# The first branch's values as pairs of half-size products, with the decays between the first pairs

## The chip, the cores and the metric

The kernel runs on one core of a Trainium2 chip. The metric is the device time of one execution in microseconds (us), as a median over runs. Engines are named as in the profile: PE (TensorE, matmuls), PEld (its weight loads), DVE (VectorE), ACT (ScalarE), POOL (GpSimd) and SP (SyncE, which issues nearly all DMAs here). SBUF is the on-chip memory, PSUM the banks into which PE writes its results.

## The reference, cut to what matters

One layer with two token mixers. A row-normalised x (1024 tokens, 1024 columns) goes through one wide input projection w_in, whose columns are cut into parts:

```python
h = rmsnorm(x, norm_g)
proj = h @ w_in
(g_q, g_k, g_v, g_gate, g_rank, s_q, s_k, s_v, s_gate, m_logits) = split(proj)

log_a = log_sigmoid(g_rank @ w_dec_up + b_dec) / 16          # the decays, per key channel
o_gla = gla_chunked(g_q, g_k, g_v, log_a)                    # first branch, 4 heads, dk 128, dv 256
o_gla = rmsnorm(o_gla, gla_norm_g) * silu(g_gate)
o_sb  = stick_breaking(s_q, s_k, s_v) * silu(s_gate)         # second branch, 8 heads, d 128
gates = sigmoid(m_logits + b_gate)
out = rmsnorm(x + (gates_a * (o_gla @ w_pa) + gates_b * (o_sb @ w_pb)) @ w_o, final_g)
```

In the first branch the cumulated decay e1 = exp(cumsum(log_a)) multiplies q, and e2 = exp(-cumsum(log_a)) multiplies k, with the sum started anew in each chunk of 64 tokens. The values g_v (4 heads of 256 columns) are used in chunks as they are.

## The kernel before, in words

All products run in a reduced-width float type (fp32r). To keep the accuracy of fp32, each operand x is cut by `split` (L152 to L154) into a high part, written by an ACT copy, and a low part, written by a DVE subtraction; a product is then three matmuls, high-high, high-low, low-high. h is kept transposed as four quarters `hq[n, e]`, by halves of the tokens (n) and by even and odd blocks of 128 rows (e), each as a high and a low tile of 128 x 4 x 512.

The kernel multiplies with w_in in two ways.

*Value units* (`proj_n`, `v_unit`). One unit takes 128 tokens and 256 columns: 8 row blocks x 3 = 24 matmuls with 256 columns each, with a block of h as the stationary operand, so that tokens lie on the partitions of the result. ACT and DVE split the result into a staging tile, and SP stores two units at a time. The line `st` holds 56 such units: three pairs of the second branch's heads (keys "s", 1 to 3; pair 0 was done while x was read), then the first branch's four heads (keys "g"), 8 units each. `store_v` writes the second branch's values to `d_v`; the first branch's go to `d_gv[h]`, as 128 tokens x 8 token blocks x (high, low) x 256 columns.

*Pairs* (`pair_job`, class `Pairs`). 256 columns of w_in are multiplied with all 1024 tokens by Strassen's scheme in Winograd's form: seven products instead of eight, each of half size in both row parity and token half, on combined operands. On the side of h these are the quarters A11, A12, A22 and the sums S1 to S4, built once and kept; on the side of w_in the four sub-blocks and the differences T1 to T4, built for every job. One product (a *unit*, numbered 0 to 6 in a job) is 4 row blocks x 3 = 12 matmuls with 512 columns each, with w_in as the stationary operand, so that the *columns of w_in* lie on the partitions of the result: the result is transposed as against a value unit's. Three PSUM banks x, y, z collect the products: units 0, 2, 4 and 6 add up in x, units 3 and 5 in z, unit 1 in y. Partial sums s1, s2 and s5 are copied out by ACT (`keep`, L260) before the bank goes on; `evict` then handles the four results (J, n): column block J, token half n. `total` (L291) adds the kept sum by DVE. `Pairs.run` also issues, at given units, the splits of the next job's weights and the load (and the four POOL subtractions for T1 to T4) of the one after that. Two raw weight buffers are there.

The order before:

1. x is read, normalised and transposed, with the values of the first pair of second-branch heads (to about 45 us).
2. The value stretch: 56 value units. Threaded between them in an order written by hand for ACT and DVE (`tc.manual_schedule`) are first the decays, then the sums for S1 to S4. The decays are seven steps: `code` (transposes of the rank code, L488), `logit` (the rank product on PE, bias by DVE, L495), `decay_a` (DVE, then Exp on ACT), `decay_b` (Ln on ACT, then DVE), `decay_c` (a scan on DVE, L507), `decay_d` (two Exp on ACT), `decay_e` (a small copy, and the stores of e1 and e2 to DRAM). Their tiles lie in the slots that later hold S1 to S4. The sums are made by POOL (L526, L529) one per unit, 32 in all, and each is split three units later. The line of sums has 36 entries.
3. 24 pair jobs, 168 units. The first 24 units run alone; the rest run four at a time between the 32 blocks (4 heads x 8 blocks of 128 tokens) of the first branch's recurrence (`gl_load`, `gl_local`, `gl_out`, `gl_gate`), and the last ones alone.
4. The second branch's attention, with gate and output projections between, then the second output projection and the final norm.

Outside of the hand-written stretches a planner orders each engine's instructions: it takes what is ready by its own cost estimates, and of several ready ones the one issued earlier in the text. On the chip each engine then works strictly through its planned list, and waits where an operand is not there. Tiles come from rings of a fixed number of buffers per tag: "f" (5 tiles of 128 x 512), "o" (3 staging tiles of 128 x 2 x 512), "tr" (2 PSUM banks for transposes), "pp" (3 PSUM banks for products).

Of the kernel before, what the change touches and what calls it, by code (L numbers as in the profile page):

```python
# [9 lines left out]
F32 = mybir.dt.float32  # L10
F32R = mybir.dt.float32r
AF = mybir.ActivationFunctionType
# [38 lines left out]
class Line:  # L51


    def __init__(self, items):
        self.items = list(items)
# [9 lines left out]
class Pairs:  # L65
# [1 line left out]

    def __init__(self, jobs):  # L70
        self.jobs = [j() for j in jobs]
        self.at = 0
# [22 lines left out]
def hybrid_layer(ctx: ExitStack, tc: tile.TileContext, x, norm_g, w_in, w_up, b_dec,  # L95
# [56 lines left out]
    def split(src, hi, lo, eng=nc.vector):  # L152
        nc.scalar.activation(hi, src, AF.Copy)  # L153
        eng.tensor_sub(lo, src, hi.bitcast(F32))  # L154

    def half(n):
        return slice(n * HALF, (n + 1) * HALF)
# [39 lines left out]
    def proj_n(ws, quads, tb, n=DV):  # L197

        pt = ps.tile([P, HALF], F32, tag="pp", name="pp", bufs=3)
        cs = slice(tb % 4 * P, (tb % 4 + 1) * P)  # L200
        for kb in range(KB):
            q = quads[tb // 4, kb % 2]
            h_, l_ = q[0][:, kb // 2, cs], q[1][:, kb // 2, cs]
            whi, wlo = ws(kb)
            nc.tensor.matmul(pt[:, 0:n], h_, whi, start=kb == 0, stop=False)  # L205
            nc.tensor.matmul(pt[:, 0:n], h_, wlo, start=False, stop=False)  # L206
            nc.tensor.matmul(pt[:, 0:n], l_, whi, start=False, stop=kb == KB - 1)  # L207
# [120 lines left out]
    def store_v(key, i, tb):  # L328

        st = vst.pop((key, tb // 2)) if tb % 2 else None  # L330
        if st is not None:
            for e in range(2):
                nc.sync.dma_start(d_v[2 * i + e][:, tb - 1:tb + 1], st[:, :, :, e * P:(e + 1) * P].bitcast(F32))

    def v_stage(key, tb):
        if tb % 2 == 0:
            vst[key, tb // 2] = (stage().rearrange("p a b -> p (a b)")
                                 .rearrange("p (t s c) -> p t s c", t=2, s=2))
        return vst[key, tb // 2][:, tb % 2]
# [91 lines left out]
        split(vraw[key][:, 4 * i:4 * i + 4], hi, lo)  # L431
        vws.setdefault(key, []).append((hi, lo))

    def v_unit(key, tb):
        nm, i = key
        st = v_stage(key, tb)
        split(proj_n(rows_of(vws[key]), hq, tb), st[:, 0], st[:, 1])
        if nm == "s":
            store_v(key, i, tb)
        elif tb % 2:  # L440
            nc.sync.dma_start(d_gv[i][:, tb - 1:tb + 1], vst.pop((key, tb // 2)).bitcast(F32))
# [21 lines left out]
    nc.sync.dma_start(wup, w_up)  # L463
    wst = slot(4, [P, GLA_H * P], "wst", F32R)
    rst = slot(5, [P, T], "rst", F32R)
    rmask = slot(7, [P, T], "rmask")
    nc.gpsimd.memset(wst.bitcast(F32), 0.0)
    nc.gpsimd.memset(rst.bitcast(F32), 0.0)
    nc.gpsimd.memset(rmask, 1.0)
    nc.gpsimd.memset(ch3(rmask)[:, :, 0:1], 0.0)  # L470
    u2 = [slot(i, [P, 2 * T], "u") for i in range(2)]
    e2 = [slot(i, [P, 2 * T], "e") for i in (2, 3)]
    U = [u2[h // 2][:, h % 2 * T:(h % 2 + 1) * T] for h in range(GLA_H)]
    E = [e2[h // 2][:, h % 2 * T:(h % 2 + 1) * T] for h in range(GLA_H)]

    def stack(dst, src, rows):
        for r0, part in zip((0, 32, 64), rows):
            if part == "h":
                nc.scalar.activation(dst[r0:r0 + RANK], src, AF.Copy)
        r0 = 32 * rows.index("l")  # L480
        nc.vector.tensor_sub(dst[r0:r0 + RANK], src, dst[0:RANK].bitcast(F32))

    def code(n):
        if n == 0:
            stack(wst, wup, "hlh")
        pt = ps.tile([P, HALF], F32, tag="tr", name="tr")
        for b in range(4):
            nc.tensor.transpose(pt[0:RANK, b * P:(b + 1) * P], rcode[:, n * 4 + b], ident)  # L488
        stack(rst[:, half(n)], pt[0:RANK, :], "hhl")

    def logit(h):
        for n in range(2):
            pt = ps.tile([P, HALF], F32, tag="tr", name="tr")
            nc.tensor.matmul(pt, wst[:, h * P:(h + 1) * P], rst[:, half(n)], start=True, stop=True)
            nc.vector.tensor_scalar(U[h][:, half(n)], pt, vcol[:, 16 + h:17 + h], None, op0=ALU.add)  # L495


    def decay_a(h):
        nc.vector.scalar_tensor_tensor(E[h], U[h], -1.0, U[h], op0=ALU.mult, op1=ALU.min)
        nc.scalar.activation(E[h], E[h], AF.Exp)  # L500

    def decay_b(h):
        nc.scalar.activation(E[h], E[h], AF.Ln, bias=1.0)
        nc.vector.scalar_tensor_tensor(E[h], U[h], 0.0, E[h], op0=ALU.min, op1=ALU.subtract)

    def decay_c(h):
        nc.vector.tensor_tensor_scan(U[h], rmask, E[h], 0.0, op0=ALU.mult, op1=ALU.add)  # L507

    def decay_d(h):
        nc.scalar.activation(E[h], U[h], AF.Exp, scale=1.0 / TAU)  # L510
        nc.scalar.activation(U[h], U[h], AF.Exp, scale=-1.0 / TAU)

    def decay_e(h):
        nc.vector.tensor_copy(ebl[:, h], ch3(E[h])[:, :, CH - 1])
        nc.sync.dma_start(d_e1[h], E[h])
        nc.sync.dma_start(d_e2[h], U[h])


    f = {}
# [33 lines left out]
    st.run(1)  # L553
    for i, s in enumerate("hl"):
        nc.sync.dma_start(d_a21[i], hq[1, 0][i].bitcast(F32))
    for fn, hs in ((code, ((0,), (1,))), (logit, ((0, 1), (2, 3))), (decay_a, ((0, 1), (2, 3))),
                   (decay_b, ((0,), (1,), (2,), (3,))), (decay_c, ((0,), (1,), (2,), (3,))),
                   (decay_d, ((0,), (1,), (2,), (3,))), (decay_e, ((0, 1, 2, 3),))):
        for group in hs:
            for h in group:  # L560
                fn(h)
            st.run(1)
    for ops in line:
        for op in ops:
            op()
# [33 lines left out]
    def merge_pair(c0, i, b0, dst):  # L599
# [14 lines left out]
    pairs = Pairs(gla_qk(0) + [gg_pair(0), merge_pair(C_MA, 0, 0, d_ga), gg_pair(1)] + gla_qk(1) +  # L614
                  [gg_pair(2), gg_pair(3)] +
                  [f for i in range(4) for f in (qk_pair(C_SQ, i, d_q), qk_pair(C_SK, i, d_k))] +
                  [merge_pair(C_MA, i, 0, d_ga) for i in range(1, 4)] +
                  [merge_pair(C_MB, i, 8, d_gb) for i in range(4)])
    pairs.run(24)


    gl_ctx = ExitStack()
# [449 lines left out]
```

## Time and profile before

| | |
|---|---|
| median of 3 runs | 1263.05 us (1262.35 to 1263.29) |
| profiled execution, its own time | 1259.98 us |
| its span (first to last instruction) | 1258.3 us |
| granted TensorE clock, mean | 0.999 |
| PE / DVE / ACT / POOL busy | 98% / 60% / 41% / 19% of the span |
| DMA | 212.09 MB, mean 169 GB/s |

The busy times come from one profiled execution. A matmul's row gives its full passage through the array, so rows of matmuls that follow each other overlap; the distance between two starts is what one costs in a row of many. "L254" is line 254 of the kernel above. A row of a group gives busy time, mean duration in ns, the idle time of the engine before its members, and what ended that idle time.

### The profile page before, as it was taken

To read this page: it belongs to the slowest core of one execution; us is meant where nothing else is said; L and a number is where in the kernel's file an instruction comes from. 1 tells how busy PE (TensorE), PEld (TensorE's weight loads), DVE (VectorE), ACT (ScalarE), POOL (GpSimd) and SP (SyncE) were. 2 spreads that over 40 slices of the span, in tenths; PEclk is the share of its full clock that TensorE was granted. 3 is DMA by queue.
4 is the path that set the end of the run, shared out by engine and by line. 5 is a ranking of instruction groups with operands and counts; after the bars stand their busy time and mean duration, and the time that the engine had idled before them with its cause. 6 is when DMAs were issued, how large, how long until landed. Compare 5 with 4: busy or idle time off the path is not lost.

```text
span 1258.3 us, 18805 instructions
## 1 busy us (share of the span) xinstructions
PE 1234.0 (98%) x6947; PEld 1054.5 (84%) x6947; DVE 753.4 (60%) x1309; ACT 519.8 (41%) x1024; POOL 243.3 (19%) x280
## 2 busy tenths in 40 slices
PE   8999999999999999999999999999999999999998
PEld 8999999888888888888888877777777878888986
DVE  5682454545667666666564357778887775444533
ACT  5454332344344444444444444545644443122322
POOL 2400471323223233232323010000100000000010
PEclk9999999999999999999999999999999999999999
DMA  7547353534644565655433765444775437543232
GB/s 270 186 142 269 126 181 133 188 116 149 192 157 137 188 208 173 215 179 177 159 117 121 246 206 160 135 163 147 220 245 175 135 109 265 190 161 110 85 116 92
DMA packets 176982, 212.09 MB, mean 169 GB/s; under 512 B 11222, under 2 KB 129004, under 8 KB 174332
## 3 DMA queue, kind: packets, MB, share of 16 engines
q1 hardware_dynamic: 175740, 209.34, 50.8%
q10 hardware_dynamic: 1152, 1.57, 0.3%
q8 instruction: 54, 0.88, 0.3%
q14 instruction: 36, 0.29, 0.1%
HBM read 133.28 MB, written 77.59 MB: 168 GB/s over the span
## 4 chain that ended last, share of the span: by engine, by line
PE 84%; DVE 8%; DMA 3%; ACT 2%; issue 2%; SPq 0%; POOL 0%; DVEq 0%; POOLq 0%; ACTq 0%
PE pp L254 12%; PE pp L256 12%; PE pp L255 12%; PE pp L207 7%; PE pp L205 7%; PE pp L206 7%; PE pp L193 6%; PE pp L194 6%; PE pp L192 5%; DVE eb L828 3%; PE av L864 1%; DVE be L833 1%; PE tr L847 1%; PE av L865 1%; PE av L863 1%
## 5 line engine op out<-in xcount | busy, mean ns | idle before, releaser
L153 ACT ACTIVATE wh<-raw 128x1024 fp32r<-128x1024 f32 x57 | 60.4, 1060 | 125.8 <-PE pp L193 69.6
L154 DVE TENSOR_TENSOR wl<-tt,wh 128x1024 fp32r<-128x1024 f32 x48 | 58.8, 1224 | 69.3 <-ACT wh L153 69.1
L291 DVE TENSOR_TENSOR f<-pp,f 128x512 f32<-128x512 f32 x72 | 49.7, 690 | 81.2 <-PE pp L256 77.9
L154 DVE TENSOR_TENSOR wl<-raw,wh 128x1024 fp32r<-128x1024 f32 x57 | 78.2, 1371 | 29.4 <-ACT wh L153 28.4
L153 ACT ACTIVATE wh<-tt 128x1024 fp32r<-128x1024 f32 x48 | 50.9, 1061 | 75.7 <-PE pp L255 69.0
L830 POOL TENSOR_SCALAR_AFFINE_SELECT be<-be 128x128 f32<-128x128 f32 x64 | 23.0, 360 | 277.1 <-ACT be L822 211.1
L828 DVE TENSOR_TENSOR_SCAN eb<-eb 128x128 f32<-128x128 f32 (+6 forms) x56 | 71.8, 1282 | 5.6 <-ACT eb L821 3.1
L154 DVE TENSOR_TENSOR o<-pp,o 128x256 fp32r<-128x256 f32 (+1 forms) x72 | 32.4, 451 | 66.1 <-ACT o L153 63.0
L153 ACT ACTIVATE o<-pp 128x256 fp32r<-128x256 f32 (+1 forms) x72 | 29.0, 403 | 93.5 <-PE pp L207 90.3
L821 ACT ACTIVATE eb<-z 128x384 f32<-128x384 f32 (+4 forms) x96 | 48.4, 506 | 44.6 <-PE z L819 30.7
L260 ACT ACTIVATE f<-pp 128x512 f32<-128x512 f32 x72 | 42.5, 590 | 55.8 <-PE pp L256 55.8
L228 POOL TENSOR_TENSOR tt<-raw 128x512 f32<-128x512 f32 x24 | 31.2, 1302 | 150.4 <-DVE wl L154 135.8
L153 ACT ACTIVATE ath<-tr 128x512 fp32r<-128x512 f32 (+2 forms) x96 | 44.0, 496 | 38.8 <-PE tr L847 37.9
L215 POOL TENSOR_TENSOR r<-r,nhalf 128x1 f32<-128x1 f32 x40 | 23.4, 586 | 188.3 <-DVE r L214 188.3
L154 DVE TENSOR_TENSOR atl<-tr,ath 128x512 fp32r<-128x512 f32 (+2 forms) x96 | 51.1, 546 | 5.3 <-ACT ath L153 5.3
L864 PE MATMUL av<-atl,v 128*128 128x256 f32 x160 | 47.0, 293 | 3.9 <-DVE atl L154 3.9
L847 PE MATMUL tr<-ident,be 128*128 128x128 f32 x288 | 44.5, 278 | 5.8 <-DVE be L833 4.9
L847 PEld LDWEIGHTS tr<-ident,be 128*128 128x128 f32 x288 | 32.5, 140 | 20.7 <-DVE be L833 11.2
L192 PE MATMUL pp<-bh,wh 128*128 128x512 f32 x128 | 49.9, 390 | 0.0
L193 PE MATMUL pp<-bl,wh 128*128 128x512 f32 x128 | 49.9, 390 | 0.0
L194 PE MATMUL pp<-bh,wl 128*128 128x512 f32 x128 | 49.9, 390 | 0.0
L833 DVE TENSOR_TENSOR be<-be,eb 128x128 f32<-128x128 f32 (+3 forms) x64 | 48.3, 755 | 1.9
(406 smaller groups left out, 4177.2 us busy)
## 6 DMA issues: line engine op xcount, KB each, us to landing
raw<-in_w_in_dram SPq DMA_DIRECT2D x31, 1024.0 KB, 5.9
d_v<-o SPq DMA_DIRECT2D x32, 256.0 KB, 3.2
d_gv<-o SPq DMA_DIRECT2D x16, 512.0 KB, 2.7
v<-d_gv SPq DMA_DIRECT2D x32, 256.0 KB, 3.1
d_q<-o SPq DMA_DIRECT2D x16, 512.0 KB, 5.7
d_k<-o SPq DMA_DIRECT2D x16, 512.0 KB, 3.9
k<-d_k SPq DMA_DIRECT2D x8, 1024.0 KB, 5.0
v<-d_v SPq DMA_DIRECT2D x8, 1024.0 KB, 6.6
```

What stands on the lines that cost most here:

```text
L153: nc.scalar.activation(hi, src, AF.Copy)
L154: eng.tensor_sub(lo, src, hi.bitcast(F32))
L192: nc.tensor.matmul(pt, whi[:, kb], h_, start=kb == 0, stop=False)
L193: nc.tensor.matmul(pt, whi[:, kb], l_, start=False, stop=False)
L194: nc.tensor.matmul(pt, wlo[:, kb], h_, start=False, stop=kb == KB - 1)
L205: nc.tensor.matmul(pt[:, 0:n], h_, whi, start=kb == 0, stop=False)
L206: nc.tensor.matmul(pt[:, 0:n], h_, wlo, start=False, stop=False)
L254: nc.tensor.matmul(pt, bh[:, j], ah[:, j], start=first and j == 0, stop=False, skip_group_check=True)
L255: nc.tensor.matmul(pt, bh[:, j], al[:, j], start=False, stop=False, skip_group_check=True)
L256: nc.tensor.matmul(pt, bl[:, j], ah[:, j], start=False, stop=j == 3, skip_group_check=True)
L828: nc.vector.tensor_tensor_scan(rest, rest, rest, om[:, T - P:T - P + 1], op0=ALU.mult, op1=ALU.min)
L847: nc.tensor.transpose(pt[:, b * P:(b + 1) * P], be[:, c:c + P], ident)
```

## The change

The first branch's values leave the value stretch and become pair jobs. `gv_pair(h)` multiplies all tokens with the 256 value columns of head h; its results lie with the columns on the partitions, so each one (128 columns x 512 tokens) is turned by four PE transposes into a "tr" bank, split by ACT and DVE, and stored by two DMAs (high and low) into the same `d_gv[h]`, in pieces of 128 columns. The turn is not issued with the eviction: it goes into a list `late`, which `Pairs.run` empties behind the next unit. The result without a kept sum (unit 6) is copied to SBUF by ACT.

The value stretch keeps the 24 units of the second branch, and only the sums for S1 to S4 between them: 25 line entries instead of 36, eight sums per 5.5 units, each split two entries later. The decays move behind the value stretch: they get their own pool of tiles `dq` (u and e with two buffers each, so heads 2 and 3 take the buffers of heads 0 and 1), run in two groups of two heads, one step behind each of the first 14 pair units, and are no longer under the hand-written order. The list of pairs begins with the values of heads 0 and 1, then q and k of heads 0 and 1, as 28 jobs in all; 35 units instead of 24 run ahead of the first branch's blocks.

```diff
 class Pairs:
-    def __init__(self, jobs):
+    def __init__(self, jobs, late):
...
+            due = self.late[:]
+            self.late.clear()
             self.jobs[i]["unit"](u)
+            for f in due:
+                f()
...
-    vjobs = [(("s", i), C_SV + i * DV) for i in range(1, SB_H // 2)] + [(("g", h), C_GV + h * DV) for h in range(GLA_H)]
+    vjobs = [(i, C_SV + i * DV) for i in range(1, SB_H // 2)]
...
-    line = [[] for _ in range(36)]
+    line = [[] for _ in range(25)]
...
-            line[8 * j + i].append(op)
+        at = [(8 * j + i) * 22 // 32 for i in range(8)]
+        for i, op in enumerate(ops):
+            line[at[i]].append(op)
         for i, nm in ((2, "S1"), (4, "S3"), (5, "S2"), (7, "S4")):
-            line[8 * j + i + 3].insert(0, part(nm, j))
+            line[at[i] + 2].insert(0, part(nm, j))
...
+    def gv_pair(h):
+        def evict(J, n, bank, add):
+            if add is None:
+                add = ev.tile([P, HALF], F32, tag="f", name="f")
+                nc.scalar.activation(add, bank, AF.Copy)
+            else:
+                total(bank, add)
+            def turn():
+                pt = ps.tile([P, HALF], F32, tag="tr", name="tr")
+                for b in range(4):
+                    nc.tensor.transpose(pt[:, b * P:(b + 1) * P], add[:, b * P:(b + 1) * P], ident)
+                o = stage()
+                split(pt, o[:, 0], o[:, 1])
+                for i in range(2):
+                    nc.sync.dma_start(d_gv[h][:, 4 * n:4 * n + 4, i, J * P:(J + 1) * P],
+                                      o[:, i].bitcast(F32).rearrange("p (b c) -> p b c", c=P))
+            late.append(turn)
+        return pair_job(w_in, C_GV + h * DV, evict)
...
+    pairs = Pairs([gv_pair(0), gv_pair(1)] + gla_qk(0) + [gg_pair(0), gg_pair(1)] + gla_qk(1) +
+                  [gv_pair(2), gg_pair(2), gv_pair(3), gg_pair(3)] + [merge_pair(C_MA, 0, 0, d_ga)] +
...
-    wup = slot(6, [RANK, GLA_H * P], "wup")
+    wup = dq.tile([RANK, GLA_H * P], F32, tag="wup", name="wup")
...
     def logit(h):
+        U[h], E[h] = (dq.tile([P, T], F32, tag=t, name=t, bufs=2) for t in "ue")
...
-    pairs.run(24)
+    djobs = [(code, (0,)), (code, (1,))]
+    for hs in ((0, 1), (2, 3)):
+        for fn in (logit, decay_a, decay_b, decay_c, decay_d, decay_e):
+            djobs.append((fn, hs))
+    for fn, hs in djobs:
+        pairs.run(1)
+        for h in hs:
+            fn(h)
+    pairs.run(35 - len(djobs))
+    dq_ctx.close()
```

More of the change, by code (lines that the diff above doesn't have):

```diff
@@ L432, in v_split, with v_unit @@
         vws.setdefault(key, []).append((hi, lo))
[L434 to L441, printed above, removed]
+    def v_unit(i, tb):
+        st = v_stage(i, tb)
+        split(proj_n(rows_of(vws[i]), hq, tb), st[:, 0], st[:, 1])
+        store_v(i, i, tb)
     def ch3(a):
@@ L458, in hybrid_layer @@
     st = Line(vline)
-    wup = slot(6, [RANK, GLA_H * P], "wup")
[L463 to L516, printed above, removed]
     f = {}
@@ L555, in hybrid_layer @@
         nc.sync.dma_start(d_a21[i], hq[1, 0][i].bitcast(F32))
[L556 to L562, printed above, removed]
     for ops in line:
@@ L613, in hybrid_layer @@
     a21_ctx.close()
-    pairs = Pairs(gla_qk(0) + [gg_pair(0), merge_pair(C_MA, 0, 0, d_ga), gg_pair(1)] + gla_qk(1) +
-                  [gg_pair(2), gg_pair(3)] +
+    late = []
+    pairs = Pairs([gv_pair(0), gv_pair(1)] + gla_qk(0) + [gg_pair(0), gg_pair(1)] + gla_qk(1) +
+                  [gv_pair(2), gg_pair(2), gv_pair(3), gg_pair(3)] + [merge_pair(C_MA, 0, 0, d_ga)] +
                   [f for i in range(4) for f in (qk_pair(C_SQ, i, d_q), qk_pair(C_SK, i, d_k))] +
                   [merge_pair(C_MA, i, 0, d_ga) for i in range(1, 4)] +
-                  [merge_pair(C_MB, i, 8, d_gb) for i in range(4)])
@@ L619, in hybrid_layer @@
-    pairs.run(24)
+                  [merge_pair(C_MB, i, 8, d_gb) for i in range(4)], late)
+    dq_ctx = ExitStack()
+    dq = dq_ctx.enter_context(tc.tile_pool(name="dq", bufs=1, reuse_waits="tile"))
+    wup = dq.tile([RANK, GLA_H * P], F32, tag="wup", name="wup")
+    nc.sync.dma_start(wup, w_up)
+    wst = dq.tile([P, GLA_H * P], F32R, tag="wst", name="wst")
+    rst = dq.tile([P, T], F32R, tag="rst", name="rst")
+    rmask = dq.tile([P, T], F32, tag="rmask", name="rmask")
+    nc.gpsimd.memset(wst.bitcast(F32), 0.0)
@@ new lines, in hybrid_layer, with stack, code @@
+    nc.gpsimd.memset(rst.bitcast(F32), 0.0)
+    nc.gpsimd.memset(rmask, 1.0)
+    nc.gpsimd.memset(ch3(rmask)[:, :, 0:1], 0.0)
+    U, E = {}, {}
+    def stack(dst, src, rows):
+        for r0, part in zip((0, 32, 64), rows):
+            if part == "h":
+                nc.scalar.activation(dst[r0:r0 + RANK], src, AF.Copy)
+        r0 = 32 * rows.index("l")
+        nc.vector.tensor_sub(dst[r0:r0 + RANK], src, dst[0:RANK].bitcast(F32))
+    def code(n):
+        if n == 0:
+            stack(wst, wup, "hlh")
+        pt = ps.tile([P, HALF], F32, tag="tr", name="tr")
+        for b in range(4):
+            nc.tensor.transpose(pt[0:RANK, b * P:(b + 1) * P], rcode[:, n * 4 + b], ident)
+        stack(rst[:, half(n)], pt[0:RANK, :], "hhl")
@@ new lines, in logit, with decay_a @@
+    def logit(h):
+        U[h], E[h] = (dq.tile([P, T], F32, tag=t, name=t, bufs=2) for t in "ue")
+        for n in range(2):
+            pt = ps.tile([P, HALF], F32, tag="tr", name="tr")
+            nc.tensor.matmul(pt, wst[:, h * P:(h + 1) * P], rst[:, half(n)], start=True, stop=True)
+            nc.vector.tensor_scalar(U[h][:, half(n)], pt, vcol[:, 16 + h:17 + h], None, op0=ALU.add)
+    def decay_a(h):
+        nc.vector.scalar_tensor_tensor(E[h], U[h], -1.0, U[h], op0=ALU.mult, op1=ALU.min)
+        nc.scalar.activation(E[h], E[h], AF.Exp)
@@ new lines, in decay_b, with decay_c, decay_d, decay_e @@
+    def decay_b(h):
+        nc.scalar.activation(E[h], E[h], AF.Ln, bias=1.0)
+        nc.vector.scalar_tensor_tensor(E[h], U[h], 0.0, E[h], op0=ALU.min, op1=ALU.subtract)
+    def decay_c(h):
+        nc.vector.tensor_tensor_scan(U[h], rmask, E[h], 0.0, op0=ALU.mult, op1=ALU.add)
+    def decay_d(h):
+        nc.scalar.activation(E[h], U[h], AF.Exp, scale=1.0 / TAU)
+        nc.scalar.activation(U[h], U[h], AF.Exp, scale=-1.0 / TAU)
+    def decay_e(h):
+        nc.vector.tensor_copy(ebl[:, h], ch3(E[h])[:, :, CH - 1])
+        nc.sync.dma_start(d_e1[h], E[h])
+        nc.sync.dma_start(d_e2[h], U[h])
```

1 line of the change is left out of this document (added).

## The prediction, made before the result was known

> **What bounds the kernel now.** I read the page first (shares by engine, the slices, the chain that ended last), then the busy time by stage, then the waits of TensorE.
>
> ```profile
> span 1258.3 us, 18805 instructions
> PE 1234.0 (98%) x6947; PEld 1054.5 (84%) x6947; DVE 753.4 (60%) x1309; ACT 519.8 (41%) x1024; POOL 243.3 (19%) x280
> PE 84%; DVE 8%; DMA 3%; ACT 2%; issue 2%; SPq 0%; POOL 0%; DVEq 0%; POOLq 0%; ACTq 0%
> ```
> ```profile
> 44.70:209.90 165.20, 165.01 (x1364) 164.07 (x1364) 82.28 (x118) 67.28 (x114) 50.79 (x39) 1.00 0.52 173
> 209.90:275.40 65.50, 65.50 (x290) 54.22 (x289) 36.65 (x50) 23.47 (x33) 24.32 (x22) 1.00 0.51 168
> 275.40:690.00 414.60, 414.60 (x2050) 341.17 (x2049) 257.69 (x549) 185.03 (x375) 121.05 (x111) 1.00 0.51 165
> ```
> ```profile
> PE pp L205 <- DVE o L154: 0.2, 1, 0.2
> ```
>
> The columns of the second fence are the stretch, its length, then the busy time of PE, PEld, DVE, ACT and POOL, the granted clock, the DMA share and GB/s. The three stretches are the value stretch (56 value units with the decays threaded in), the first pairs, and the pairs with the first branch's blocks between them. In all three TensorE is busy for the whole length at clock 1.00, and the third fence is the only wait of PE between 44.7 and 690 us: 0.2 us. So up to 690 us the time is the sum of what TensorE issues, and VectorE (50%, 56% and 62% of these stretches) and ScalarE (41%, 36%, 45%) cost nothing until they make it wait. Nothing after 690 us is touched by the diff, so I take it as unchanged.
>
> **TensorE's work, by pace.** A matmul's listed duration includes its pipeline, so I go by the distance between starts.
>
> ```profile
> 149.77 0.28 PE L207 MATMUL pp<-wh,ha12l 128*128 128x256 f32 x1
> 152.65 0.28 PE L207 MATMUL pp<-wh,ha22l 128*128 128x256 f32 x1
> ```
> ```profile
> 242.31 0.39 PE L254 MATMUL pp<-S4h,dh 128*128 128x512 f32 x1
> 245.03 0.39 PE L254 MATMUL pp<-ha22h,wh 128*128 128x512 f32 x1
> ```
> ```profile
> 19.01 1.03 PE L393 MATMUL tr<-ident,xs 128*128 128x128 f32 x8
> 19.80 0.37 PE L205 MATMUL pp<-vw,ha12h 128*128 128x272 f32 x1
> 20.01 0.29 PE L206 MATMUL pp<-vw,ha12h 128*128 128x272 f32 x1
> 20.14 0.29 PE L207 MATMUL pp<-vw,ha12l 128*128 128x272 f32 x1
> ```
>
> The first two rows are 24 matmuls apart, one value unit: 2.88 us. The next two are 12 apart, one half-size product with 512 columns: 2.72 us. From the last fence, eight transposes and the first matmul behind them take 20.01 - 19.01 = 1.00 us, where that matmul alone takes 20.14 - 20.01 = 0.13: 0.87 for eight.
>
> - Removed: 4 heads x 8 units x 2.88 = 92.2 us.
> - Added: 4 jobs x 7 products x 2.72 = 76.2 us.
> - Added: 4 heads x 4 results x 4 transposes = 64, so 64/8 x 0.87 = 7.0 us.
> - Kept, only moved: the eight small transposes of the rank code and the eight logit matmuls.
>
> Net 92.2 - 76.2 - 7.0 = 9.0 us less for TensorE. This is the bound on the good side.
>
> **What must hide, and where it may not.** First the shorter value stretch. It now holds 24 units, 24 x 2.88 = 69 us, and GpSimd must make all 32 sums for S1 to S4 in it.
>
> ```profile
> L529 POOL TENSOR_TENSOR f<-f 128x512 f32<-128x512 f32 x16 | 24.1, 1508 | 18.1 <-DVE S3l L154 12.0 <-DVE S2l L154 5.5
> 184.84 1.30 POOL L529 TENSOR_TENSOR f<-f 128x512 f32<-128x512 f32 x1
> 205.02 0.69 DVE L154 TENSOR_TENSOR S4l<-f,S4h 128x512 fp32r<-128x512 f32 x1
> ```
>
> At 1.5 us each they are 48 of 69 us, and the written order lets the last sum stand three units (8 us) ahead of its split. Before, the last sum was made 20 us before its split used it (second and third row). The margin shrinks but stays positive, and S4 is wanted only in the sixth product of the first pair: I cost it at nothing; if GpSimd fell 5 us behind, the manual order on ACT and DVE would hold evictions and cost those few us.
>
> Second, the decays. They leave a manual order, threaded between value units that ask VectorE for only 0.42 us each, and go between the units of the first pairs, which ask for more.
>
> ```profile
> L507 DVE TENSOR_TENSOR_SCAN u<-rmask,e 128x1024 f32<-128x1024 f32 x4 | 9.1, 2282 | 0.0
> L495 DVE TENSOR_SCALAR u<-tr,vcol 128x512 f32<-128x512 f32 x8 | 5.8, 748 | 0.6 <-PE tr L494 0.6
> L504 DVE SCALAR_TENSOR_TENSOR e<-u,e 128x1024 f32<-128x1024 f32 x4 | 4.9, 1218 | 1.9 <-ACT e L503 1.9
> L499 DVE SCALAR_TENSOR_TENSOR e<-u 128x1024 f32<-128x1024 f32 x4 | 4.7, 1218 | 0.0
> L154 DVE TENSOR_TENSOR o<-pp,o 128x256 fp32r<-128x256 f32 x20 | 8.4, 419 | 13.4 <-ACT o L153 11.1 <-DMA wup<-in_w_dec_up_dram 2.1
> ```
> ```profile
> L511 ACT ACTIVATE u<-u 128x1024 f32<-128x1024 f32 x4 | 4.2, 1058 | 0.1
> L503 ACT ACTIVATE e<-e 128x1024 f32<-128x1024 f32 x4 | 4.2, 1058 | 0.0
> L503 ACT ACT_TABLE_LOAD x1 | 1.3, 1283 | 0.0
> ```
> ```profile
> L154 DVE TENSOR_TENSOR wl<-tt,wh 128x1024 fp32r<-128x1024 f32 x48 | 58.8, 1224 | 69.3 <-ACT wh L153 69.1
> L291 DVE TENSOR_TENSOR f<-pp,f 128x512 f32<-128x512 f32 x72 | 49.7, 690 | 81.2 <-PE pp L256 77.9
> L154 DVE TENSOR_TENSOR ha11l<-tr,ha11h x4: 684/691/692, 9.6 to 24.8; 128x512 fp32r<-128x512 f32 x4
> L153 ACT ACTIVATE wh<-tt 128x1024 fp32r<-128x1024 f32 x48 | 50.9, 1061 | 75.7 <-PE pp L255 69.0
> L260 ACT ACTIVATE f<-pp 128x512 f32<-128x512 f32 x72 | 42.5, 590 | 55.8 <-PE pp L256 55.8
> ```
>
> One value pair asks VectorE for three weight splits and a half one (3.5 x 1.22), three sums (3 x 0.69) and four turned results, each like an x eviction from the transposes' bank (4 x 0.69): 9.1 us of its 7 x 2.72 + 4 x 0.44 = 20.8 us. ScalarE has 3.5 x 1.06, four copies of 0.59 and four of the turned (0.59 also): 8.4 us. Either is under half. The four heads' decays add 9.1 + 5.8 + 4.9 + 4.7 = 24.5 us on VectorE, and on ScalarE four passes of 4.2 and some four or five table loads of 1.28 (two chains of two heads each switch Exp to Ln and back), 22 to 23 us. Were all of it done in the 14 units it is written between (two pairs, 41.6 us), VectorE would need 2 x 9.1 + 24.5 = 42.7 and ScalarE 39 to 40: full. It need not be. The two buffers of u and of e keep heads 2 and 3 back until heads 0 and 1 are stored, and their result is wanted only at the seventh pair; so this work spreads over some three and a half pairs, 70 us, at some 80% of VectorE.
>
> What stays are bursts. decay_d for two heads is a table load and four Exp, 1.28 + 4 x 1.06 = 5.5 us; two scans are 4.6 us; Ln for two heads 3.4 us. A copy queued behind one is late. The third product goes on in the bank that s1 is copied from, the fifth in that of s2 and the sixth in that of s5, with one other product between: each copy has 2.72 us less its own 0.59, 2.1 us of slack. The fifth product's sum is read from the bank in which the seventh goes on: 2.72 - 0.69 = 2.0 us. So a burst can hold TensorE by up to 5.5 - 2.1 = 3.4, 3.4 - 2.1 = 1.3 and 4.6 - 2.0 = 2.6 us: 7.3 us a chain, 14.6 us for the two. That is the outer bound; the inner is zero, as TensorE's own order is planned and may take the next product into another bank. A tight copy follows three of seven products, a tight sum one of seven, and a burst that hits is half over on average: (3.4 + 1.3) x 3/7 / 2 + 2.6 / 7 / 2 = 1.2 us a chain, 2.4 for both. I take 2.5 us.
>
> Third, the stores and the round trip of the decays.
>
> ```profile
> d_v<-o SPq DMA_DIRECT2D x32, 256.0 KB, 3.2
> d_gv<-o SPq DMA_DIRECT2D x16, 512.0 KB, 2.7
> f<-d_e SPq DMA_DIRECT2D x16, 256.0 KB, 3.9
> d_e<-u SPq DMA_DIRECT2D x4, 512.0 KB, 5.7
> ```
>
> d_gv is now written by 32 transfers of 256 KB in pieces of 128 columns, as d_v is (3.2 us to landing): 16 more issues on SP, spread over four pairs, and read no sooner than three pairs later. Nothing. The decays' store and reload, 5.7 + 3.9 = 9.6 us, now stand close to their reader, the second product of the third pair, some 2 x 20.8 + 2 x 2.72 = 47 us in. The chain for heads 0 and 1 is, by the rows, 4 x 0.75 + 3.5 (two sums, one Exp) + 4.6 (load, two Ln, one sum) + 4.6 (scans) + 2.1 (last two Exp) + 9.6 = 27 us, with the code and its weights some 35: 12 us to spare, so no term, but waiting behind the pair's own work can eat it.
>
> Four further pair jobs and turns between the first branch's blocks ask no more of DVE than the query and key pairs that run there now without a wait. Sum: 9.0 - 2.5 = 6.5 us less. The profiled execution took 1259.98 us, so 1253.5 by its own time; it lies 3.1 us under the median of the three runs, 1263.05, and on that scale the forecast is 1256.5 us.
>
> **Rivals.** (a) Everything is hidden: the full 9.0 us, 1254. For it: 0.2 us of waits in 645 us, with VectorE at 62% where the blocks run. Against: no stretch there has bursts of 4 to 5 us. 20%.
>
> (b) The decays' bursts hold TensorE in most of the places where they can: stalls of 7 to 11 us cancel the gain, 1261 to 1265. For it: DVE and ACT are both near full if the decays keep their written places. 13%.
>
> (c) The decays of heads 0 and 1 reach their reader late. VectorE then waits in order on the reload of e, with the next sums and weight splits queued behind it; TensorE, after the two or three products that the banks allow, waits for them. Price: the lateness less some 8 us. It decides once the chain takes over 47 + 8 + 9 = 64 us in place of 35; at the 54 us that it took before for all four heads between value units it costs nothing.
>
> ```profile
> 50.19 1.28 ACT L479 ACTIVATE wst<-wup 16x512 fp32r<-16x512 f32 x2 [0.58 <-DMA wup<-in_w_dec_up_dram]
> 104.05 0.42 DVE L514 COPY ebl<-e 128x16 f32<-128x16 f32 x4
> ```
>
>  With the bursts on top, stalls of 14 us, so 5 us above the median of before: 1268. 12%.
>
> (d) Transposes that do not follow each other closely.
>
> ```profile
> L847 PE MATMUL tr<-ident,be 128*128 128x128 f32 x288 | 44.5, 278 | 5.8 <-DVE be L833 4.9
> ```
>
> A transpose lasts 278 ns. Were each paid in full, 64 would cost 17.8 us and not 7.0, and the net gain would be 16.0 - 17.8 = -1.8: slower, 1265 before any stall. The eight in 0.79 us above speak against it. [...] 2%.
>
> **How the numbers follow.** The forecast (stalls of 1 to 6 us, 1255 to 1260) has 53%, (a) 20, (b) 13, (c) 12, (d) 2. Faster by over 0.2% (2.5 us, about what a measurement of this kernel can tell from no change) takes the forecast, (a), and a slip of the forecast's edge away: 71%. Same: most of (b), 14%. Slower: (c), (d) and the rest, 15%. The range runs from just beyond the full gain, 1252.5, to 1264, into (b); the likeliest case's own is 1255 to 1260.
>
> **What would show it.** Right: matmul spacing of products unchanged; a value stretch of about 69 us from 45 to 114 us with no wait; the sum of PE's idle time between 114 and 190 us at 1 to 6 us, put down to ACT f or DVE f; four table loads or more there. Wrong: idle over 9 us in that stretch (b); DVE waiting on f<-d_e (c); groups of four transposes that take over 0.8 us (d); or a pair's unit that starts late on S or tt parts, which would mean the short value stretch was not free.

## The result, and the profile after

The changed kernel takes 1270.43 us (median of 4, 1268.98 to 1271.53) against 1263.17 us: ratio 1.0057, 95% interval 1.0041 to 1.0073. A second comparison gave 1268.66 against 1262.07 us, ratio 1.0045 (1.0030 to 1.0061). It is slower by some 7 us where 6.5 us less were forecast. Its profiled execution took 1268.98 us.

The page of the changed kernel, its first row, the busy times and the chain that ended last:

```profile
span 1267.0 us, 18177 instructions
...
PE 1230.3 (97%) x6579; PEld 1033.8 (82%) x6579; DVE 771.7 (61%) x1313; ACT 539.9 (43%) x1038; POOL 272.7 (22%) x296
...
PE 82%; DVE 8%; DMA 4%; ACT 3%; issue 3%; SPq 0%; DVEq 0%; POOLq 0%; POOL 0%; ACTq 0%
```

TensorE has less to do than before and waits more. Where, show the busy times by stage (value stretch, first 35 pair units, pairs with the first branch's blocks; columns as before: length, PE, PEld, DVE, ACT, POOL, granted clock):

```profile
44.70:114.30 69.60, 69.60 (x580) 69.42 (x580) 40.60 (x50) 25.34 (x48) 51.57 (x34) 1.00 0.55 166
114.30:235.70 121.40, 111.80 (x494) 90.11 (x492) 77.82 (x98) 67.13 (x86) 38.73 (x33) 0.97 0.54 176
235.70:690.00 454.30, 454.30 (x2245) 374.23 (x2245) 276.11 (x575) 200.13 (x398) 133.47 (x120) 1.00 0.55 174
```

The value stretch ends at 114.3 us, after 69.6 us, with no hole: the shorter stretch for S1 to S4 was free, as predicted. Between the blocks there is no hole either. The loss ahead of the attention is in the second row alone: 121.4 - 111.8 = 9.6 us of PE idle, and a clock of 0.97. These are the waits of PE from 114 to 190 us (what waits, for what; total, number, longest):

```profile
PE tr L557 <- DVE o L159: 5.3, 1, 5.3
PE pp L259 <- ACT f L265: 1.8, 1, 1.8
PE tr L616 <- DVE o L159: 1.6, 1, 1.6
PE tr L616 <- DVE rst L602: 0.5, 1, 0.5
PE tr L557 <- DVE f L296: 0.4, 1, 0.4
```

L557 is a turn's transposes, L616 a logit product, L259 a pair's product. What holds that product is seen on ScalarE, from 129 to 148 us (start, duration; L622 and L632/L633 are Exp, L625 is Ln, L265 the copy of a partial sum):

```profile
129.26 0.58 ACT L265 ACTIVATE f<-pp 128x512 f32<-128x512 f32 x1
129.74 1.05 ACT L622 ACTIVATE e<-e 128x1024 f32<-128x1024 f32 x1
130.81 1.28 ACT L625 ACT_TABLE_LOAD   x1
132.10 1.06 ACT L625 ACTIVATE e<-e 128x1024 f32<-128x1024 f32 x1
133.18 1.28 ACT L622 ACT_TABLE_LOAD   x1
134.47 1.06 ACT L622 ACTIVATE e<-e 128x1024 f32<-128x1024 f32 x1
135.55 1.28 ACT L625 ACT_TABLE_LOAD   x1
136.85 1.06 ACT L625 ACTIVATE e<-e 128x1024 f32<-128x1024 f32 x1
...
140.85 1.28 ACT L632 ACT_TABLE_LOAD   x1
142.14 1.06 ACT L632 ACTIVATE e<-u 128x1024 f32<-128x1024 f32 x1
144.18 1.06 ACT L632 ACTIVATE e<-u 128x1024 f32<-128x1024 f32 x1 [0.97 <-DVE u L629]
145.14 1.99 ACT L633 ACTIVATE u<-u 128x1024 f32<-128x1024 f32 x2
147.03 0.58 ACT L265 ACTIVATE f<-pp 128x512 f32<-128x512 f32 x1
```

From 129.3 to 147.6 us ScalarE is idle for 1 us. The planner takes Ln of one head as soon as its Exp is done, ahead of the Exp of the next head, so the table changes four times per pair of heads, not two. The last row is the copy of s1, which empties bank x for the next product; it stands behind a table load and four Exp. TensorE's side, from 145 us:

```profile
145.38 0.50 PE L616 MATMUL tr<-rst,wst 128*128 128x512 f32 x1 [1.59 <-DVE o L159]
147.66 0.57 PE L259 MATMUL pp<-S2h,wh 128*128 128x512 f32 x1 [1.78 <-ACT f L265]
148.03 0.63 PE L260 MATMUL pp<-S2l,wh 128*128 128x512 f32 x1
148.46 0.63 PE L261 MATMUL pp<-S2h,wl 128*128 128x512 f32 x1
```

The product before ended at 143.8 us. The product in the second row waits for that copy, with one logit matmul in the hole (first row): 1.6 + 1.8 = 3.4 us of idle time. Then its matmuls follow at 0.43 us, not at 0.227. The granted clock of the two stretches behind the waits, of 4.1 and 4.3 us, is down:

```profile
147.60:151.70 4.10, 4.04 (x11) 3.19 (x12) 3.64 (x3) 1.44 (x3) 4.02 (x4) 0.58 1.03 305
175.70:180.00 4.30, 4.24 (x15) 3.61 (x16) 4.27 (x9) 3.11 (x4) 1.84 (x2) 0.66 0.77 269
```

The shortfall of the clock times the length, an estimate, gives (1 - 0.58) x 4.1 = 1.7 us and (1 - 0.66) x 4.3 = 1.5 us that are lost besides the waits. The half clock lasts here from 147.9 to 151.3 us, 3.4 us at a granted clock of 0.51. How long a hole must be for it is not shown; in the second profile of the kernel before, below, it stands behind one of 2.0 us. Nor is it fixed which hole is followed by it. In the second profile of the changed kernel (the run after_again) the same two waits of 1.6 and 1.8 us are there and cost no clock; the hole of 5.3 us cost more, half clock up to 180.1 us, which is 4.2 us of work at half clock, so 2.1 us lost:

```profile
147.60:151.70 4.10, 4.03 (x18) 3.22 (x19) 3.66 (x3) 2.05 (x4) 4.02 (x4) 1.00 1.01 266
173.30:180.10 6.80, 4.21 (x12) 3.56 (x13) 6.77 (x11) 5.63 (x7) 1.81 (x2) 0.50 0.70 236
```

The longest wait, at 170 us, is one of the turns. It needs a "tr" bank, and by the order of the two banks that is the one which the turn at 162.0 us filled. ScalarE wrote the high part of that result at 164.06 us. In VectorE's order the low part stands behind the second head's step on Ln, for which VectorE idles 3.3 us, and behind the two scans for heads 2 and 3:

```profile
164.06 0.59 ACT L158 ACTIVATE o<-tr 128x512 fp32r<-128x512 f32 x1
```
```profile
169.42 1.23 DVE L626 SCALAR_TENSOR_TENSOR e<-u,e 128x1024 f32<-128x1024 f32 x1 [3.32 <-ACT e L625]
170.56 4.47 DVE L629 TENSOR_TENSOR_SCAN u<-rmask,e 128x1024 f32<-128x1024 f32 x2
174.95 0.67 DVE L159 TENSOR_TENSOR o<-tr,o 128x512 fp32r<-128x512 f32 x1
```
```profile
170.08 0.39 PE L260 MATMUL pp<-ha12l,wh 128*128 128x512 f32 x1
175.76 1.08 PE L557 MATMUL tr<-ident,f 128*128 128x128 f32 x4 [5.29 <-DVE o L159]
```

So of the 9.6 us, 3.4 belong to a hole that the copy behind four Exp ends, and 5.3 to a split behind two scans that were themselves late.

The account in the trace: first score matmul at 736.6 us against 732.1, so +4.5 us up to there; the end +8.8 us. Most of the rest, 3.9 us, comes up in the attention, whose instructions on TensorE, VectorE, ScalarE and GpSimd stand in the same order as before.

### The profile page after: what moved, and what is told of

Its sections match the earlier page's. It is cut to its first block, busy times and chain, and to the rows that moved or that the text cites. A ratio compares the mean times of both kernels' runs of the same rounds, so it can differ in the third digit from the quotient of the medians.

```text
span 1267.0 us, 18177 instructions
## 1 busy us (share of the span) xinstructions
PE 1230.3 (97%) x6579; PEld 1033.8 (82%) x6579; DVE 771.7 (61%) x1313; ACT 539.9 (43%) x1038; POOL 272.7 (22%) x296
## 4 chain that ended last, share of the span: by engine, by line
PE 82%; DVE 8%; DMA 4%; ACT 3%; issue 3%; SPq 0%; DVEq 0%; POOLq 0%; POOL 0%; ACTq 0%
PE pp L259 13%; PE pp L261 13%; PE pp L260 13%; PE pp L198 6%; PE pp L199 6%; PE pp L197 5%; PE pp L212 5%; PE pp L210 5%; PE pp L211 5%; DVE eb L858 3%; PE av L894 1%; DVE be L863 1%; DMA raw<-d_ogl 1%; PE tr L877 1%; PE av L895 1%
## 5 line engine op out<-in xcount | busy, mean ns | idle before, releaser
L296 DVE TENSOR_TENSOR f<-pp,f 128x512 f32<-128x512 f32 x84 | 58.0, 691 | 94.3 <-PE pp L261 89.9
L159 DVE TENSOR_TENSOR wl<-tt,wh 128x1024 fp32r<-128x1024 f32 x56 | 69.6, 1244 | 74.5 <-ACT wh L158 74.3
L159 DVE TENSOR_TENSOR wl<-raw,wh 128x1024 fp32r<-128x1024 f32 x57 | 83.4, 1464 | 28.6 <-ACT wh L158 26.8
L158 ACT ACTIVATE wh<-tt 128x1024 fp32r<-128x1024 f32 x56 | 59.4, 1060 | 84.2 <-PE pp L260 81.3
L233 POOL TENSOR_TENSOR tt<-raw 128x512 f32<-128x512 f32 x28 | 37.4, 1334 | 214.7 <-DVE wl L159 152.3
L265 ACT ACTIVATE f<-pp 128x512 f32<-128x512 f32 x84 | 49.6, 591 | 68.2 <-PE pp L261 68.2
L852 ACT ACTIVATE be<-z 128x384 f32<-128x384 f32 (+4 forms) x96 | 48.8, 510 | 0.0
L893 PE MATMUL av<-ath,v 128*128 128x256 f32 x160 | 46.6, 291 | 1.4 <-ACT ath L158 1.4
```

## The experiments

Each starts from the changed kernel unless it says otherwise. "First score" is the start of the first score matmul of the attention, the end of all that the change touches, in the profiled execution. The 13.5 us that the expectations call waits are more than the waits, which are 9.6 us: 13.5 equals the 4.5 us by which the first score matmul came late and the 9.0 us by which it was to come early.

| run | first score | time (before on the same chip) | ratio, 95% interval |
|---|---|---|---|
| before, two profiles | 732.1, 732.1 us | 1263.17; 1261.77, one run (1262.18) | |
| changed, two profiles | 736.6, 737.2 us | 1270.43 (1263.17), 1268.66 (1262.07) | 1.0057, 1.0045 |
| nodecay | 723.9 us | 1256.55 (1262.18) | 0.9956 (0.9941 to 0.9971) |
| noact | 726.4 us | 1258.14, one run (1262.81) | |
| batch | 738.6 us | 1271.38 (1262.18) | 1.0071 (1.0056 to 1.0086) |
| late2 | 732.8 us | 1266.64 (1262.81) | 1.0023 (1.0011 to 1.0034) |
| spread_planned | 730.5 us | 1260.91 (1262.81) | 0.9980 (0.9969 to 0.9990) |
| spread | 726.1 us | 1258.73 (1262.18) | 0.9967 (0.9953 to 0.9981) |
| spread_late2 | 725.3 us | 1256.20 (1262.07) | 0.9949 (0.9929 to 0.9969) |
| pieces | 732.2 us | 1263.89 (1262.81) | 1.0002 (0.9992 to 1.0011) |

**The value pairs without the decays.**

```diff
-        U[h], E[h] = (dq.tile([P, T], F32, tag=t, name=t, bufs=2) for t in "ue")
+        U[h] = E[h] = dq.tile([P, T], F32, tag="u", name="u", bufs=2)
...
-        for fn in (logit, decay_a, decay_b, decay_c, decay_d, decay_e):
+        for fn in (logit, None, None, None, None, decay_e):
...
```

> The changed kernel with the four middle steps of the decays (decay_a to decay_d: Exp, Ln, scan, Exp) left out; the rank code, the logits and the stores stay, and the logits are stored in place of e1 and e2. Theory A (the decays' passes on ScalarE and VectorE, with eight table loads, hold TensorE among the first pairs): the waits of 13.5 us between 114 and 190 us are gone but for 1 us or less, and the span up to the last pair product is 9 us shorter than before; time 1255 to 1259. Theory B (the value pairs themselves do it: the turned transposes behind a late eviction, with two banks): waits of 5 us or more remain, time over 1262.

The first score matmul comes at 723.9 us, 8.2 us ahead of before, and 0.5 us of waits is left of 9.6. Busy times from 112 to 182 us, of the changed kernel and then of this one:

```profile
112.00:182.00 70.00, 60.40 (x277) 48.17 (x276) 51.38 (x56) 49.27 (x60) 17.84 (x15) 0.95 0.43 140
```
```profile
112.00:182.00 70.00, 69.52 (x335) 57.30 (x334) 39.72 (x64) 27.66 (x43) 19.98 (x21) 1.00 0.62 201
```

The same engines with 21.6 us less on ScalarE and 11.7 less on VectorE get 58 more matmuls done in the same 70 us. Turns, stores and value pairs run alongside each other with that 0.5 us of waits; theory B falls, and the decays cost 736.6 - 723.9 = 12.7 us: 9.1 us of waits, 3.2 of clock, and 0.4 that neither shows.

**ScalarE's part alone.**

```diff
-        nc.scalar.activation(E[h], E[h], AF.Exp)
...
-        nc.scalar.activation(E[h], E[h], AF.Ln, bias=1.0)
...
-        nc.scalar.activation(E[h], U[h], AF.Exp, scale=1.0 / TAU)
-        nc.scalar.activation(U[h], U[h], AF.Exp, scale=-1.0 / TAU)
```

> The changed kernel without the decays' ScalarE passes (the two Exp, the Ln and the third Exp of each head are left out); their VectorE steps, scans included, stay. If ScalarE's bursts are what holds TensorE, the waits between 114 and 190 us fall from 13.5 to under 3 us. If the scans on VectorE (two of 2.28 us, one behind the other) do it, 5 us or more remain.

The first score matmul is at 726.4 us: 10.2 of the 12.7 us go with ScalarE's passes. VectorE's steps alone cost 2.5 us, and all waits left, 3.2 us where under 3 were expected, are:

```profile
PE tr L557 <- DVE u L617: 1.6, 1, 1.6
PE tr L557 <- DVE f L296: 1.1, 1, 1.1
PE tr L616 <- DVE rst L602: 0.5, 1, 0.5
```

The scans are still there, still two in a row (4.46 us, at 135.9 and at 156.9 us), but 3.8 and 13.7 us earlier than in the changed kernel, and VectorE no longer idles for a Ln ahead of them, where it did for 2.9 and 3.3 us. So the 5.3 us behind the scans needed both engines.

**Fewer table loads.** u and e of two heads lie in one tile; ScalarE passes over both at once.

```diff
+        if h % 2:
+            nc.scalar.activation(E2[h - 1], E2[h - 1], AF.Exp)
...
+        if h % 2 == 0:
+            nc.scalar.activation(E2[h], E2[h], AF.Ln, bias=1.0)
...
```

> The changed kernel with u and e of two heads side by side in one tile each, so that ScalarE makes one pass over 2048 columns for both heads in each of Exp, Ln, Exp, Exp: three table switches per group at most in place of four, and the same columns. If the switching between Exp and Ln from head to head is the main cause, two table loads of 1.28 us and their order are saved per group and the waits fall from 13.5 to some 6 us, time 1261 to 1265. If the bursts as such are the cause, passes of 2.1 us are no better than two of 1.06 and the time stays within 2 us of 1270.

Four table loads instead of eight, 5.1 us less on ScalarE, and no gain: 738.6 us. The waits, 8.4 us with one of 0.5 us as before, are 1.2 us less and mostly at the copy now:

```profile
PE pp L259 <- ACT f L265: 6.8, 3, 3.6
PE tr L618 <- DVE o L159: 1.1, 1, 1.1
```

The clock took that back: it is at half from 145.7 to 152.5 us and from 183.2 to 190.0 us, of which TensorE works 5.4 us in each, so 5.4 us are lost in place of 3.2. So the count of loads is not the cause by itself: the waits did not fall to the 6 us expected of that. The passes that a copy stands behind are 1.9 us each here, in place of 1.06.

**Turns two units late.**

```diff
-            due = self.late[:]
-            self.late.clear()
+            self.late.append(None)
+            due = self.late[:self.late.index(None)]
+            del self.late[:len(due) + 1]
...
-    late = []
+    late = [None]
```

> The changed kernel with each turn issued two units behind its eviction in place of one. Theory A (bursts of the decays hold the copies and the splits): the hold on the copy of s2 at 145 us stays, the one of 5.5 us at 170 us at a turn becomes shorter by one unit (2.7 us) at most; time 1266 to 1271. Theory B (turns placed too close): the waits fall from 13.5 us to 5 or less, time under 1263.

732.8 us, 3.8 us better than the changed kernel, time 1266.64: within theory A's bounds for the time, but the long wait is not shortened so much as moved, from a turn to a product whose sum is not out of its bank, because VectorE idles 2.7 us for the second Ln ahead of that sum. The two longest waits:

```profile
PE pp L260 <- DVE f L297: 3.6, 1, 3.6
PE pp L260 <- ACT f L266: 1.5, 1, 1.5
```

The clock shows in this run's times as well: the two fastest of its ten executions, 1262.56 and 1262.76 us, have a mean granted clock of 0.998 and 0.999, the other eight, 1265.63 us and more, 0.992 to 0.996.

**Decays spread, in a written order.** The values of all four heads come first, then q and k; each step of one head stands behind a unit of its own, and 49 units in place of 35 run ahead of the first branch's blocks.

```diff
-    pairs = Pairs([gv_pair(0), gv_pair(1)] + gla_qk(0) + [gg_pair(0), gg_pair(1)] + gla_qk(1) +
-                  [gv_pair(2), gg_pair(2), gv_pair(3), gg_pair(3)] + [merge_pair(C_MA, 0, 0, d_ga)] +
+    pairs = Pairs([gv_pair(h) for h in range(GLA_H)] + gla_qk(0) + [gg_pair(0), gg_pair(1)] + gla_qk(1) +
+                  [gg_pair(2), gg_pair(3)] + [merge_pair(C_MA, 0, 0, d_ga)] +
...
-            djobs.append((fn, hs))
+            djobs += [(fn, (h,)) for h in hs]
+    manual = ExitStack()
+    manual.enter_context(tc.manual_schedule(engines={mybir.EngineType.Activation, mybir.EngineType.DVE}))
...
```

> The changed kernel with the values of all four heads as the first four pairs, the decays one step of one head behind each of the first 26 units, ScalarE and VectorE in the written order through these, and 49 units ahead of the first branch's blocks. Theory A: each unit has at most one scan or two Exp behind its own eviction, so no wait over 1 us is left; table loads fall to four before the sigmoids; the span up to the last pair product is 8 to 9 us shorter than before, time 1255 to 1259. Theory B: the 16 turns remain, with waits of 5 us or more, time over 1262.

726.1 us and 1258.73, faster than before, by 6.0 us at the first score matmul where 8 to 9 were expected. The table loads are four, as expected. Two waits are left from 114 to 190 us, one of them over 1 us:

```profile
PE tr L557 <- DVE f L296: 2.3, 2, 1.3
```

**The same places, the planner's order.** The two lines with "manual" are left out again.

> As the run that spread the decays (values of four heads first, one step of one head behind each of 26 units), but with the planner's own order on ScalarE and VectorE in place of the written one. If it is the places that matter, the waits among the first pairs stay at some 3 us as there and the time at 1257 to 1260. If the written order matters, the planner bunches the steps again as soon as they are ready, waits come back to 8 us or more, time 1264 or over.

730.5 us: the bunch on ScalarE between 130 and 147 us is back, with its four loads, and so are 5.1 us of waits:

```profile
PE pp L259 <- ACT f L265: 2.7, 2, 1.3
PE tr L557 <- DVE f L296: 1.9, 1, 1.9
PE tr L616 <- DVE rst L602: 0.5, 1, 0.5
```

Neither expectation holds whole: the places alone bring 6.1 us (736.6 to 730.5) and the written order 4.4 more (to 726.1). Of these, 2.8 us are waits; the other 1.7 us are clock, at half for 3.4 us from 150.9 us on in this run and not in the other.

**Both, and turns two units late.**

> The spread decays in the written order, with each turn issued two units behind its eviction. All waits of that run among the first pairs (2.5 us) were turns that waited for the sum of the eviction one unit before, on VectorE behind a scan. With two units they should be gone: the first score matmul at 724 us in place of 726.1, time 1256 to 1258. If another wait takes their place (f tiles held longer, splits behind one another), no gain: 1258 to 1260.

725.3 us and 1256.20: the lowest median of the study, as expected for the time, though the first score matmul is 1.3 us behind the 724 expected and one wait came in the place of the two, `PE pp L260 <- DVE f L297: 1.7`. Its interval overlaps that of the run with turns one unit late.

**The attention.** The kernel before, once more; the changed kernel, once more; and the kernel before with the first branch's values stored as the change stores them:

```diff
-            nc.sync.dma_start(d_gv[i][:, tb - 1:tb + 1], vst.pop((key, tb // 2)).bitcast(F32))
+            st = vst.pop((key, tb // 2))
+            for e in range(2):
+                nc.sync.dma_start(d_gv[i][:, tb - 1:tb + 1, :, e * P:(e + 1) * P],
+                                  st[:, :, :, e * P:(e + 1) * P].bitcast(F32))
```

> The kernel before, unchanged, profiled a second time. In the changed kernel the attention stage (first to last score matmul) took 295.0 us against 291.0 us in the profiled execution of before, with the same instructions in the same order. If that stage varies from execution to execution with the landing of transfers, it comes out here at something other than 291.0, by 1 to 4 us; if the 4 us belong to the change, it comes out at 291.0 within 0.5 us.

> The changed kernel, unchanged, profiled a second time. The waits among the first pairs are set by the order and come back: the first score matmul at 736.6 us within 0.3. The attention stage behind it, 295.9 us from the first to the end of the score matmuls in the first profile, is set by landings and comes back at anything from 292 to 298, as in the other kernels.

> The kernel before with the first branch's values stored as the changed kernel stores them: 32 transfers of 256 KB in pieces of 128 columns in place of 16 of 512 KB in whole rows; nothing else. If the number or the shape of these transfers shifts the landing of later ones, the attention stage becomes some 2 us longer as in the changed kernels (293.5 to 298 us against 291 and 293.7) and the time 1264 to 1265. If not, no change: 1262 within 1.

First and last start of the score matmuls, in the order before, before again, changed, changed again, pieces:

```profile
L817 PE MATMUL z<-k,q x96: 278/394/505, 732.1 to 1023.1; 128*128 128x384 f32 x24, 128*128 128x512 f32 x24, 128*128 128x256 f32 x16, 128*128 128x320 f32 x16
```
```profile
L817 PE MATMUL z<-k,q x96: 278/397/499, 732.1 to 1024.9; 128*128 128x384 f32 x24, 128*128 128x512 f32 x24, 128*128 128x256 f32 x16, 128*128 128x320 f32 x16
```
```profile
L847 PE MATMUL z<-k,q x96: 277/396/697, 736.6 to 1031.5; 128*128 128x384 f32 x24, 128*128 128x512 f32 x24, 128*128 128x256 f32 x16, 128*128 128x320 f32 x16
```
```profile
L847 PE MATMUL z<-k,q x96: 278/396/500, 737.2 to 1031.9; 128*128 128x384 f32 x24, 128*128 128x512 f32 x24, 128*128 128x256 f32 x16, 128*128 128x320 f32 x16
```
```profile
L820 PE MATMUL z<-k,q x96: 277/400/502, 732.2 to 1027.4; 128*128 128x384 f32 x24, 128*128 128x512 f32 x24, 128*128 128x256 f32 x16, 128*128 128x320 f32 x16
```

The attention took 291.0 and 292.8 us before, 294.9 and 294.7 changed, 295.2 with the stores in pieces; in the other runs 292.6 (batch) to 297.2 (nodecay). The part ahead of it comes back at 732.1 us twice for the kernel before. For the changed kernel it comes 0.6 us later, where 0.3 was expected: a logit product waits 1.5 us there for a buffer of u that is still being stored.

Two things lengthen the attention. One is the clock. In the second profile of the kernel before it falls to half behind a wait of 2.0 us for ScalarE; in the first profile the wait at this place is 1.7 us, and the clock stays at 1.00:

```profile
893.20:896.60 3.40, 3.40 (x11) 2.62 (x10) 2.85 (x7) 0.81 (x2) 0.44 (x2) 0.50 1.05 402
```

TensorE works through these 3.4 us, so they cost 1.7 us, which is the difference of the two profiles but for 0.1. So the stage does vary from execution to execution, but here by the clock and not, as was expected, by the landing of transfers. Both profiles of the changed kernel have one such stretch too, from 898.9 and from 828.6 us, batch has one, nodecay 10.2 us of half clock and the run with pieces none. The other is transfers that land late, such as a q block that the changed kernel waits 1.6 us for, where the kernel before waits 0.4. Less the lost clock the attention is 291.0 and 291.1 us before, 293.2 and 293.0 changed, 290.9 in batch, 291.0 in spread_planned and 295.2 in pieces. So 1.7 us of the 3.9 are clock and some 2 us remain. Batch and spread_planned store the values in the same pieces and do not have these 2 us, so the stores alone do not bring them; the run pieces, whose 1263.89 us lies between the two times expected and whose ratio allows at most 1.4 us more than before (0.9992 to 1.0011), can't exclude a part. Whether the 2 us belong to the changed kernel or to the executions that were profiled stays open.

## Why the prediction was wrong

*TensorE's floor: right.* 9.0 us less was the sum; without the decays' middle steps 8.2 us is measured, and 0.5 us of waits are left in that run. Transposes follow each other closely (rival (d) is out): in the turn at 136.93 us of the changed kernel the next matmul starts 0.35 us behind the first of the four, where one lasts 0.27 us. Products keep their 0.227 us: the 12 matmuls from 179.20 us on take 2.72 us.

*The short value stretch, the stores, the pairs between the blocks: right,* all three at nothing. *Rival (c)* did not come: VectorE waited for the stores of u (4.6 us, as heads 2 and 3 wait for the buffers), without cost to TensorE in the first profile and with 1.5 us in the second; for the reload of e VectorE waited 2.8 us in all, and TensorE not at all.

*The bursts: the kind of wait right, the places and the chances wrong, by a factor of five.* This is the step that failed: "(3.4 + 1.3) x 3/7 / 2 + 2.6 / 7 / 2 = 1.2 us a chain, 2.4 for both. I take 2.5 us." Measured are 12.7 us. Four things were wrong in it. First, its list of tight places has the copies and the sums of products, but not the "tr" banks that turns and logit products share; the longest wait, 5.3 us, came there, for a split behind two scans. Second, it took the bursts as separate, with gaps that let copies through, and weighed each hit at half; in the trace ScalarE's passes of Exp and Ln, their table loads and the pair's own copies between them make one stretch of 18 us with 1 us of idle time. The copy of s1 in the first chain was hit in full: the hole has 1.6 + 1.8 = 3.4 us of idle time, just the 5.5 - 2.1 us that the sum multiplied by 3/14. Third, it counted "four or five table loads"; there are eight, because the planner sorts by what is ready and changes between Exp and Ln from head to head, and VectorE idled 2.9 and 3.3 us for the second Ln ahead of its scans (halving the loads, with longer passes, took only 1.2 us off the waits). Fourth, it had no term for the clock, 3.2 us in the first profile and 2.1 in the second. The outer bound, 14.6 us, held, with 10 us of waits and these 3; as it has neither the turns nor the clock in it, that is luck. The prediction's own warning, that both engines are near full if the decays keep their written places, was the better reading. Its rival (b), with 13%, was the nearer case: its 7 to 11 us hold the waits, though not the clock, and its sign, idle over 9 us in this stretch, is the one that came.

*"Nothing after 690 us is touched by the diff, so I take it as unchanged": right of the instructions, not of the time.* The attention varies, 291.0 to 297.2 us in the twelve profiles, with the landing of its transfers (0.4 us of waits for a q block in the first profile of before, 1.6 us in that of the changed kernel) and with the clock (1.7 us between the two profiles of before), and the profile of before had the shortest one of all twelve, with the clock at 1.00 through the attention. So a profiled execution at 1259.98 us, 3 us under its median, was the hint: the scale for the sum was not certain to 3 us.

*How the choice should have gone.* The sum of 39 to 43 us of work on each of two engines within 41.6 us left no room, and it was set aside because heads 2 and 3 start late. But the planned order has the decays of heads 0 and 1 first, and with the pairs' own copies they fill ScalarE for 18 us, 1 us of it idle. Working out one chain in order of time, and not by chances, would have shown that the copy of s1 does meet the four Exp, and a turn's split the scans.

## What to carry to other kernels

Work moved from a stage where evictions are short (0.42 us of VectorE) to one where a bank must be emptied within one product (2.72 us here) is priced by what stands ahead of one copy or one split in its engine's order, the waits for the other engine included, and not by its share of the engine. If a planner orders the engine by readiness, give such work its places by hand, one short step behind each unit: the best run is then 725.3 - 723.9 = 1.4 us behind the run without the decays (the two differ also in the order of the pairs and in when the turns come), and not 12.7, and the change gains 0.5%. Lost clock can come on top of a hole on TensorE: by the estimate above 1.7 us behind one of 2.0 us (the kernel before, second profile) and 1.5 and 2.1 us behind the one of 5.3 us (the changed kernel, both profiles), but none behind the waits of 1.6 and 1.8 us in the changed kernel's second profile, where 1.7 us went in the first. A difference between two single profiles can be just that, as 1.7 of the 1.8 us between those of the kernel before.

## What the hardware showed that was not expected

VectorE's split of raw weights takes 1.22 us in most of its calls. In 15 of the 57 calls of the changed kernel it takes 1.5 to 2.35 us, each with an addition or subtraction of GpSimd at the same time; three calls with over 1 us of one beside them still took 1.23 us. One long split of the changed kernel, and what GpSimd does at the same time:

```profile
149.08 2.35 DVE L159 TENSOR_TENSOR wl<-raw,wh 128x1024 fp32r<-128x1024 f32 x1
```
```profile
149.07 1.28 POOL L234 TENSOR_TENSOR tt<-raw,tt 128x512 f32<-128x512 f32 x1
150.43 2.16 POOL L236 TENSOR_TENSOR tt<-raw,tt 128x512 f32<-128x512 f32 x1
```

In the spread kernel three of the four scans took 2.76 to 3.01 us instead of 2.28; GpSimd was at work throughout two of them. This adds to VectorE's load in the first pairs beyond the sum of the prediction, with splits of 2.34, 2.35 and 2.32 us at 121, 149 and 180 us; it was not measured by itself, and no run here shows that GpSimd's work is the cause.
